# Spreading gamma over the partitions of an RMSNorm-Swish kernel with a TensorE product in place of a shuffle

## The chip, the cores and the metric

The kernel runs on one core of one Trainium2 chip. The metric is device microseconds of one execution, the median over runs. The granted TensorE clock is 1.0, and every profile is one profiled execution. In the profiles SP, ACT, DVE, POOL and PE are SyncE, ScalarE, VectorE, GpSimd and TensorE; an engine name with a q, as ACTq, is its queue of issued work.

## The reference

```python
batch, seq, dim = 16, 1024, 512          # x: 16 x 1024 x 512 float32, gamma: 512 ones, eps 1e-5
def reference(x, gamma, eps):
    rms = np.sqrt(np.mean(x ** 2, axis=-1, keepdims=True) + eps)
    x_norm = x / rms * gamma
    return (x_norm * (1.0 / (1.0 + np.exp(-x_norm)))).astype(np.float32)
```

33.56 MB are read and 33.56 MB are written.

## The kernel before

The 16384 rows lie 128 to a partition. They are cut into 11 tiles of 4 to 16 rows for each partition, in a ring of 96 rows, and into 32 chunks of 4 rows. For each chunk ACT squares (one row with a running sum, three into PSUM), DVE sums those three, POOL adds eps and takes the power -1/2 into `rstd`, DVE scales the four rows by `rstd` and gamma, and ACT applies Silu in place. SP issues the loads, ACT the stores.

```python
    sizes = [4, 4, 8] + [16] * 6 + [8, 8]
    ring = 96
    cn = 4                                        # rows of a chunk
    # ...
    gamma4 = sbuf("gamma4", [P, D])
    gamma_sb = sbuf("gamma_sb", [P, D])
    sq = [nc.alloc_psum_tensor(f"sq{i}", [P, 4, D], fp32).ap() for i in range(2)]
    # ... POOL
    nc.gpsimd.memset(gamma4, 0.0).then_inc(s_zero, 1)
    # ... for each chunk: the add (aeps), then the power (rstd)
    # ... ACT: the scratch write, then gamma into partitions 0, 32, 64 and 96
    need(nc.scalar.dma_start(out=scratch, in_=blank), s_blank, 1).then_inc(s_scratch, 16)
    need(
        nc.scalar.dma_start(out=gamma4[0:P:32, :], in_=gamma.partition_broadcast(4)),
        s_zero, 1,
    ).then_inc(s_gld, 16)
    # ... DVE
    for k in range(K + 1):
        if k < K:
            sums(k)
        if k == 0:
            need(nc.vector.stream_shuffle(gamma_sb, gamma4, [0] * 32), s_gld, 16
            ).then_inc(s_gamma, 1)
        if k == 1:
            nc.vector.wait_ge(s_gamma, 1)
        if k >= 1:
            norm(k - 1)                           # four scalings, the first waits for rstd
```

## Time and profile before

| | before |
|---|---|
| time | 160.27 us median (160.11 to 160.32) |
| span of the profiled execution | 158.7 us |
| DVE, ACT, POOL busy | 87%, 79%, 41% |
| the two DMA queues, share of the 16 engines | 49.9% + 49.3% |
| gamma lands, first scaling | 11.01, 13.31 us |
| last store issued, landed | 150.11, 158.66 us |

The time of a run is some 1.36 us longer than the landing of its last store (160.02 for the profiled execution, 158.66 its last landing).

### The profile page before, as it was taken

What the parts mean: (1) busy time and instruction counts of PE and PEld (TensorE: products, weight loads), DVE (VectorE), ACT (ScalarE), POOL (GpSimd) and SP (SyncE); (2) the same over time, 40 slices, a digit from 0 to 9 for tenths busy, and PEclk for the clock granted to TensorE, in tenths of its full rate; (3) what the DMA queues carried; (4) which work ended last, traced back from release to release, by engine and by line L of the source; (5) the groups of instructions that cost most, each with busy time, mean ns of one, the idle gap of its engine ahead of it and who ended that gap; (6) DMA issues with size and microseconds to landing.
All of it is one profiled execution on the core that took longest, in us unless ns stands there. A gap on an engine that the chain in (4) does not pass through costs nothing.

```text
span 158.7 us, 439 instructions
## 1 busy us (share of the span) xinstructions
DVE 138.9 (87%) x162; ACT 125.3 (79%) x129; POOL 65.4 (41%) x71
## 2 busy tenths in 40 slices
DVE  0249999999999999999999999999999999999300
ACT  0935989888888889988888888888998888883600
POOL 2035444444455555544444445555544444445000
DMA  7999999999999999999999999999999999999997
GB/s 235 427 523 405 396 450 419 409 452 407 460 394 413 467 421 452 413 396 479 432 413 429 446 429 413 425 417 458 429 454 396 434 446 438 446 413 438 388 458 301
DMA packets 3324, 67.15 MB, mean 423 GB/s; under 512 B 501, under 2 KB 501, under 8 KB 505
## 3 DMA queue, kind: packets, MB, share of 16 engines
q1 hardware_dynamic: 1584, 33.56, 49.9%
q10 hardware_dynamic: 1736, 33.57, 49.3%
q14 instruction: 4, 0.02, 0.0%
HBM read 33.56 MB, written 33.56 MB: 423 GB/s over the span
## 4 chain that ended last, share of the span: by engine, by line
DVE 85%; DMA 5%; ACT 1%; issue 1%; POOL 0%; POOLq 0%
DVE xb L224 53%; DVE ms L213 32%; DMA gamma<-in_gamma_dram 5%; ACT xb L184 1%; DVE gamma_sb L237 0%; POOL gamma L142 0%; POOL blank L141 0%; POOLq L65 0%
## 5 line engine op out<-in xcount | busy, mean ns | idle before, releaser
L224 DVE SCALAR_TENSOR_TENSOR xb<-xb,rstd,gamma_sb 128x512 f32<-128x512 f32 x128 | 87.4, 748 | 0.0
L184 ACT ACTIVATE xb<-xb 128x2048 f32<-128x2048 f32 x32 | 61.1, 1909 | 17.8 <-DVE xb L224 17.8
L213 DVE TENSOR_REDUCE ms<-sq 128x3 f32<-128x1536 f32 x32 | 56.1, 1754 | 7.0 <-ACT sq L172 7.0
L147 POOL TENSOR_SCALAR aeps<-ms 128x4 f32<-128x4 f32 x32 | 20.6, 644 | 75.2 <-DVE ms L213 75.2
L172 ACT ACTIVATE sq<-xb 128x1536 f32<-128x1536 f32 x32 | 45.9, 1433 | 0.0
L154 POOL TENSOR_TENSOR rstd<-aeps,neg_half 128x4 f32<-128x4 f32 x32 | 44.0, 1376 | 2.7
L165 ACT ACTIVATE junk<-xb 128x512 bf16<-128x512 f32 x32 | 19.7, 615 | 3.4 <-DMA xb<-in_x_dram 3.3
L165 ACT ACTIVATION_READ_ACCUMULATOR junk<-xb 128x1 f32 x32 | 6.0, 186 | 0.0
L199 ACT ACT_TABLE_LOAD x1 | 1.3, 1283 | 3.6 <-issue 3.6
L237 DVE LOAD_MASK_SELECT gamma_sb<-gamma x1 | 0.0, 14 | 2.3 <-DMA gamma<-in_gamma_dram 2.3
L141 POOL MEMSET blank<- 128x16 f32 x1 | 0.1, 111 | 1.5 <-POOLq L65 1.5
L237 DVE STREAM_SHUFFLE gamma_sb<-gamma 128x512 f32<-128x512 f32 x1 | 0.7, 717 | 0.0
L142 POOL MEMSET gamma<- 128x512 f32 x1 | 0.5, 524 | 0.0
L264 POOL MEMSET const-float32-0.0<- 128x1 f32 x1 | 0.1, 98 | 0.2 <-issue 0.2
L264 POOL MEMSET const-bfloat16-1.0<- 128x1 bf16 x1 | 0.1, 102 | 0.0
L264 POOL MEMSET const-uint8-127<- 128x1 uint8 x1 | 0.1, 101 | 0.0
L143 POOL MEMSET neg_half<- 128x4 f32 x1 | 0.1, 101 | 0.0
L264 POOL MEMSET const-float32-1.0<- 128x1 f32 x1 | 0.1, 98 | 0.0
## 6 DMA issues: line engine op xcount, KB each, us to landing
xb<-in_x_dram SPq DMA_DIRECT2D x6, 4096.0 KB, 41.9
out_dram<-xb ACTq DMA_DIRECT2D x6, 4096.0 KB, 31.1
xb<-in_x_dram SPq DMA_DIRECT2D x3, 2048.0 KB, 35.0
out_dram<-xb ACTq DMA_DIRECT2D x3, 2048.0 KB, 10.7
xb<-in_x_dram SPq DMA_DIRECT2D x2, 1024.0 KB, 5.8
out_dram<-xb ACTq DMA_DIRECT2D x2, 1024.0 KB, 20.8
scratch<-blank ACTq DMA_DIRECT2D x1, 8.0 KB, 7.7
gamma<-in_gamma_dram ACTq DMA_DIRECT2D x1, 8.0 KB
```

Source lines behind the costliest of these rows:

```text
L141: nc.gpsimd.memset(blank, 0.0).then_inc(s_blank, 1)
L142: nc.gpsimd.memset(gamma4, 0.0).then_inc(s_zero, 1)
L147: nc.gpsimd.tensor_scalar(out=aeps[:, k, :], in0=ms[:, k, :], scalar1=eps_f, scalar2=None, op0=ALU.add,),
L154: nc.gpsimd.tensor_tensor(out=rstd[:, k, :], in0=aeps[:, k, :], in1=neg_half, op=ALU.pow),
L165: acc = nc.scalar.activation(out=junk[k % 2], in_=xb[:, at + n_sq, :], func=AF.Square, scale=inv_d**0.5, accum_out=ms[:, k, n_sq : n_sq + 1],)
L172: square = nc.scalar.activation(out=sq[k % 2][:, 0:n_sq, :], in_=xb[:, at : at + n_sq, :], func=AF.Square, scale=inv_d**0.5,)
L184: nc.scalar.activation(out=rows, in_=rows, func=AF.Silu), s_norm, k + 1
L199: nc.scalar.preload_act_table_set("silu_and_others")
L213: nc.vector.tensor_reduce(out=ms[:, k, 0:n_sq], in_=sq[k % 2][:, 0:n_sq, :], op=ALU.add, axis=mybir.AxisListType.X,),
L224: ins = nc.vector.scalar_tensor_tensor(out=row, in0=row, scalar=rstd[:, k, j : j + 1], in1=gamma_sb, op0=ALU.mult, op1=ALU.mult,)
L237: nc.vector.stream_shuffle(gamma_sb, gamma4, [0] * 32), s_gld, 16
L264: nc = _bacc.Bacc("TRN2", target_bir_lowering=False, num_devices=1)
```

## The change

Its intent: gamma is fetched once and not four times, POOL no longer zeroes a 128x512 tile ahead of the transfer, and the spread over the partitions is a product of a column of ones with the row of gamma, written to the fourth row of a PSUM buffer of which the squares use three, and copied out by DVE.

```diff
-    gamma4 = sbuf("gamma4", [P, D])
+    gamma1 = sbuf("gamma1", [1, D])
+    ones = sbuf("ones", [1, P])
...
-    nc.gpsimd.memset(gamma4, 0.0).then_inc(s_zero, 1)
+    nc.gpsimd.memset(ones, 1.0).then_inc(s_one, 1)
...
-    need(
-        nc.scalar.dma_start(out=gamma4[0:P:32, :], in_=gamma.partition_broadcast(4)),
-        s_zero, 1,
-    ).then_inc(s_gld, 16)
+    nc.scalar.dma_start(out=gamma1, in_=gamma.unsqueeze(0)).then_inc(s_gld, 16)
...
+    spread = sq[1][:, 3, :]
+    nc.tensor.wait_ge(s_one, 1)
+    need(
+        nc.tensor.matmul(spread, lhsT=ones, rhs=gamma1, start=True, stop=True),
+        s_gld, 16,
+    ).then_inc(s_spread, 1)
...
-                nc.vector.stream_shuffle(gamma_sb, gamma4, [0] * 32), s_gld, 16
+                nc.vector.tensor_copy(out=gamma_sb, in_=spread), s_spread, 1
```

(Declarations of semaphores are left out.)

More of the change, by code (lines that the diff above doesn't have):

```diff
@@ L86 @@
     s_gld = nc.alloc_semaphore("s_gld")
-    s_zero = nc.alloc_semaphore("s_zero")
+    s_one = nc.alloc_semaphore("s_one")
+    s_spread = nc.alloc_semaphore("s_spread")
     s_half = nc.alloc_semaphore("s_half")
```

## The prediction

> **What bounds the kernel now.** I read the page first (busy times and the 40 slices), then the chain of waits that ended last, then the timeline of the start, then the DMA issues and the stretches at the end.
>
> ```profile
> span 158.7 us, 439 instructions
> DVE 138.9 (87%) x162; ACT 125.3 (79%) x129; POOL 65.4 (41%) x71
> ...
> DMA  7999999999999999999999999999999999999997
> ...
> q1 hardware_dynamic: 1584, 33.56, 49.9%
> q10 hardware_dynamic: 1736, 33.57, 49.3%
> ```
>
> There are two candidates for the bound. DVE is busy for 87% of the span. The 16 DMA engines are busy too: the two queues (q1 the loads, q10 the stores, the scratch write and gamma) add up to 99.2% of their time, and no slice after the first is below nine tenths. The chain of waits names DVE:
>
> ```profile
> 2.50 8.51 DMA gamma<-in_gamma_dram
> 11.01 0.03 issue
> 11.04 0.72 DVE gamma_sb L237 x2
> 11.76 0.06 DVE ms L213
> 11.82 1.49 issue
> 13.31 2.73 DVE xb L224 x4
> ...
> 142.84 5.31 DVE xb L224 x8
> 148.15 0.02 issue
> 148.17 1.91 ACT xb L184
> ```
>
> The reader is to see that gamma opens this chain. The transfer is issued at 2.50 and lands at 11.01; the shuffle over the partitions (0.72) follows at once; then come the second reduction and the first scaling at 13.31, and from there DVE runs without a pause (its groups show 0.0 us idle before the scalings) to 148.15. By this view whatever is added between 11.01 and 13.31 arrives at the end one for one.
>
> But the chain ends with the last Silu at 150.08, and the span ends 8.6 us later. What lies there is the last store, and the DMA issues, asked for by stretch (130 to 140, 140 to 150, 150 to 155 us), show that it waits in a queue:
>
> ```profile
> out_dram<-xb ACTq DMA_DIRECT2D x1, 4096.0 KB, 14.5
> ...
> out_dram<-xb ACTq DMA_DIRECT2D x1, 2048.0 KB, 10.7
> ...
> out_dram<-xb ACTq DMA_DIRECT2D x1, 2048.0 KB, 8.6
> ...
> 145.00:150.00 5.00, 3.14 (x5) 3.74 (x2) 0.06 (x1) 1.00 0.92 393
> ...
> 152.00:154.00 2.00, 0.00 (x0) 0.00 (x0) 0.00 (x0) 1.00 1.09 467
> 154.00:156.00 2.00, 0.00 (x0) 0.00 (x0) 0.00 (x0) 1.00 1.03 442
> ```
>
> (The last number of a DMA issue is the time from issue to landing; the last two of a stretch are the DMA share and GB/s.) The timeline has these three stores issued at 134.52, 143.15 and 150.11, so they land at 149.0, 153.85 and 158.7. The last two gaps are 4.85 us each for 2.10 MB, which is 432 GB/s, the rate of the whole run. So each store starts when the one before it is through, and the DMA engines, never idle since about 1 us, are what sets the end. The DVE chain runs close beside them with a little slack: in the packet records of the trace the last store's first data starts between 152.69 and 153.43 on the different engines, 2.6 to 3.3 us after its issue at 150.11. Some of that is start-up: the very first load, which had no queue before it, was issued at 0.00 and its first packet starts at 1.00. I estimate 1.0 to 1.5 us for the store[...]. The slack of the DVE chain is then 2.6 - 1.5 = 1.1 us at least and 3.3 - 1.0 = 2.3 at most, 1.7 in the middle.
>
> [...] q10 has 1736 packets, which is 11 stores of 128 + 16, the scratch write of 128 + 16, and 8 left for gamma, 4 of data and 4 of completion[...]. [...] The kernel before has no TensorE instruction[...].
>
> **The change part by part.** *Removed:* the 128x512 memset on POOL (0.52 us, done at 2.47) and the wait of the gamma transfer on it. It held the issue back by about 0.1 us (the scratch issue ends at 2.39, gamma's starts at 2.50). *The issue itself* took 1.10 us on ACT against 0.34 for a store; one plain row may be cheaper, up to 0.76 us, but then ACT only waits for the first load (its first square starts at 4.93, that load landed at 4.80 by the semaphore record). Worth 0.1 us, and DVE waits for gamma later anyhow.
>
> *The landing* hardly moves. In the packet records gamma stands on each ring behind the scratch write, whose completion packets start at 9.17 to 9.39; gamma's data follow at 9.85 to 10.00 and its completions at 10.54 to 10.68, each with one 0.61 us packet of the loads in between. So it lands two turns behind scratch[...]. [...] scratch's spread over all 16 is 0.2 us. I take 11.0, give or take 0.3.
>
> *Added on the path:* the product. [...] *Replaced on the path:* the shuffle (0.72, and 0.01 for its mask) by a copy of 128x512 out of PSUM. One pass of DVE over 128x512 takes 0.72 to 0.75 in this trace, so I take 0.70: -0.03. The product writes the fourth bank of a buffer of which only three are used, so no square is held up.
>
> Sum on DVE: 0.0 + 2.1 - 0.03 = about +2.1 us; the first scaling starts at 15.4 in place of 13.31, and the last store is issued at 152.2 in place of 150.11.
>
> *At the end of the span:* loads do not depend on DVE until the ring of 96 rows is full, and both queues hold work without a break, so during the 2 us the engines carry loads instead of stores and total work is the same. The other late stores have more room: the 4096 KB one is issued at 134.52 and its predecessor lands at 139.3, the next is issued at 143.15 and its predecessor at 149.0. Only the last one is near: 2.1 of delay less 1.1 to 2.3 of slack leaves 0 to 1.0, in the middle 0.4. Result: 160.27 + 0.4 = 160.7 us.
>
> **The rivals.** (a) *One for one.* The chain of waits is right, the store costs the same 8.6 us after its issue, and the kernel goes to 160.27 + 2.1 = 162.4 us. For it: the chain itself. Against it: the 4.85 us rhythm of the last landings and the 99.2%. (b) *Fully absorbed:* start-up of a store is 1.0 us or less of those 2.6 and the product is at most 1.6 us; 160.2 to 160.3. For it: the middle of my slack is close to the delay. (c) *Faster:* gamma comes earlier. DVE sat idle for 2.26 us before the shuffle, and the first row of rstd was ready at 10.2, so DVE could gain up to some 2 us; but the DMA engines would not end earlier for it, so even this makes 160.2. The packet order speaks against it. (d) *Gamma in pieces:* if one row were cut into 4-byte pieces, 32 for each engine, every piece behind a load packet of 0.6 to 1.2 us, gamma would land 20 to 38 us late, far over any slack, and the kernel would take about 180 to 198. [...] I give it 2%.
>
> **Range and chances.** The bottom is DMA work that does not change, 160.0 with the scatter of 160.11 to 160.32; the top is rival (a), 162.4. Two per cent is 3.2 us, so slower than 163.5 needs a product of over 3 us with no slack, or (d): 0.03. Faster than 157.1 would need less DMA work: 0.01. Within 2%: 0.96.
>
> **What would show it.** In the changed profile: a gamma landing at 10.7 to 11.3; TensorE busy for 1.7 to 2.2 us in one place just after it; DVE's idle time before the copy up from 2.3 to about 4.4; first scaling near 15.4; last store issued near 152.2 and landing in 6.5 to 7 us in place of 8.6; DMA share of the two queues still 98 to 99%. If the last store still takes 8.6 us, or the landings before it move back by 2 us as well, the DMA bound is wrong and (a) right. If gamma lands beyond 12, the reading of the packet order is wrong.

The 432 and 423 GB/s are what the trace shows, and that no higher rate is possible it does not show. The sum was: 0.0 for the landing, 2.1 for the product, -0.03 for the copy, so +2.1 us on DVE; less 1.7 us of slack that is 0.4 us, and 160.27 + 0.4 = 160.7 us. The 2.1 us, and the 1.7 to 2.2 us under what would show it, no trace had shown by then; the profile after shows 2.08 us.

## More of the kernel before

The experiments ran on three chips, which their results number 0, 8 and 9; for the first measurement of the changed kernel the chip is not recorded. Each chip served one session, so chip and session can't be told apart.

One more group of before will be needed, POOL's add of eps (columns: busy us, mean ns of one, idle time before them):

```profile
L147 POOL TENSOR_SCALAR aeps<-ms 128x4 f32<-128x4 f32 x32 | 20.6, 644 | 75.2 <-DVE ms L213 75.2
```

It is an operation on four elements for each partition, and it takes 0.64 us in the mean. The first one, at a time when DVE is idle, takes 0.23.

## The result and the profile after

The changed kernel takes 161.18 us (160.84 to 161.37, four runs) against 160.27 (160.11 to 160.32). The ratio is 1.0056, with a 95% interval of 1.0037 to 1.0075: a small loss, clear of noise, inside the predicted range and 0.5 us above the predicted 160.7.

The head of the page and the two queues, after:

```profile
span 159.5 us, 443 instructions
...
PE 2.1 (1%) x2; PEld 0.5 (0%) x2; DVE 138.9 (87%) x161; ACT 125.2 (78%) x129; POOL 104.2 (65%) x71
...
q1 hardware_dynamic: 1584, 33.56, 49.7%
q10 hardware_dynamic: 1730, 33.57, 49.0%
```

The product is there with 2.1 us, no square of ACT waits for it (0.0 us idle before L174), DVE has as much work as before, and the DMA queues still fill 98.7% of the span. Two things are not as predicted. POOL is busy for 104 us in place of 65. And q10 has 1730 packets, which is 1728 for the stores and the scratch write and only 2 for gamma: one packet of 2048 bytes and one completion, so one engine carried it. The trace's record of the issue has gamma as 1x1 elements of 2048 bytes. In the kernel before it has 4x1, and gamma took 4 packets of 2048 bytes and 4 completions there.

The chain of waits after (start, duration, what), its beginning and its end:

```profile
2.43 8.18 DMA gamma<-in_gamma_dram
...
10.65 2.08 PE sq L213 x2
...
12.75 0.69 DVE gamma_sb L244
...
13.50 1.52 issue
...
142.89 1.68 DVE ms L220
...
144.64 2.66 POOL aeps L149
...
147.37 1.04 POOL rstd L156
...
148.44 2.75 DVE xb L231 x4
...
151.21 1.91 ACT xb L186
```

At the beginning the product takes 2.08 us and the copy 0.69, gamma landed 0.4 us earlier than before (10.60 in place of 11.01), and the first scaling starts at 15.03 in place of 13.31: +1.72. At the end something new has appeared. Before, the last eight scalings ran in one piece. Now the last four wait for POOL, whose add took 2.66 us; its group shows that this is no single case:

```profile
L149 POOL TENSOR_SCALAR aeps<-ms 128x4 f32<-128x4 f32 x32 | 68.3, 2133 | 39.8 <-DVE ms L220 39.8
```

By the timeline the first adds take 0.66 us, and from the ninth chunk on (45.4 us) each takes 2.65: it ends only when all four scalings that DVE runs meanwhile are over. Where a text below says that POOL is shut out, it means such an add of 2.65 us and nothing beyond it. In the middle of the kernel nobody waits for it, since `rstd` is needed one chunk later. At the end DVE has no reduction left to do, and the last scaling waits 1.24 us. So the last store is issued at 153.15, 3.04 us later than before: 1.72 from the start, 1.24 from POOL, and 0.08 of small change.

The end of the span after, by stretches (the last two columns are DMA share and GB/s), and the last store's line:

```profile
150.00:152.00 2.00, 0.00 (x0) 0.00 (x0) 1.18 (x2) 0.79 (x1) 0.00 (x0) 1.00 1.09 467
152.00:154.00 2.00, 0.00 (x0) 0.00 (x0) 0.00 (x0) 1.12 (x1) 0.00 (x0) 1.00 0.42 180
154.00:156.00 2.00, 0.00 (x0) 0.00 (x0) 0.00 (x0) 0.00 (x0) 0.00 (x0) 1.00 1.21 508
```

```profile
out_dram<-xb ACTq DMA_DIRECT2D x1, 2048.0 KB, 6.3
```

Between 152 and 154 us the DMA share falls to 0.42: here, and only here, the engines have run out of work (they run dry) and wait for the last store to be issued. (A packet counts where it begins, so a share above 1 in the next stretch is no error.) In the packet records all 16 engines begin that store between 153.99 and 154.14, together, 0.84 to 0.99 us after its issue; before, they began it one by one, from 152.69 to 153.43, as each was through with the store ahead. The store lands 6.3 us after its issue in place of 8.6. Of 3.04 us of delay, 2.2 were absorbed in its queue and 0.82 reached the end (159.48 in place of 158.66).

### The profile page after: what moved, and what is told of

It reads as the page before. It is cut to its first block, busy times and chain, and to the rows that moved or that the text cites. A ratio compares the mean times of both kernels' runs of the same rounds, so it can differ in the third digit from the quotient of the medians.

```text
span 159.5 us, 443 instructions
## 1 busy us (share of the span) xinstructions
PE 2.1 (1%) x2; PEld 0.5 (0%) x2; DVE 138.9 (87%) x161; ACT 125.2 (78%) x129; POOL 104.2 (65%) x71
## 3 DMA queue, kind: packets, MB, share of 16 engines
q10 hardware_dynamic: 1730, 33.57, 49.0%
## 4 chain that ended last, share of the span: by engine, by line
DVE 83%; DMA 5%; POOL 2%; PE 1%; issue 1%; ACT 1%; ACTq 0%; POOLq 0%
DVE xb L231 52%; DVE ms L220 31%; DMA gamma<-in_gamma_dram 5%; POOL aeps L149 2%; PE sq L213 1%; ACT xb L186 1%; POOL rstd L156 1%; DVE gamma_sb L244 0%; ACTq L194 0%; POOL blank L143 0%; POOLq L65 0%
## 5 line engine op out<-in xcount | busy, mean ns | idle before, releaser
L149 POOL TENSOR_SCALAR aeps<-ms 128x4 f32<-128x4 f32 x32 | 68.3, 2133 | 39.8 <-DVE ms L220 39.8
L231 DVE SCALAR_TENSOR_TENSOR xb<-xb,rstd,gamma_sb 128x512 f32<-128x512 f32 x128 | 88.6, 785 | 1.2 <-POOL rstd L156 1.2
L220 DVE TENSOR_REDUCE ms<-sq 128x3 f32<-128x1536 f32 x32 | 57.2, 1789 | 7.0 <-ACT sq L174 7.0
L174 ACT ACTIVATE sq<-xb 128x1536 f32<-128x1536 f32 x32 | 45.9, 1433 | 0.0
L156 POOL TENSOR_TENSOR rstd<-aeps,neg_half 128x4 f32<-128x4 f32 x32 | 35.5, 1110 | 2.7
L244 DVE COPY gamma_sb<-sq 128x512 f32<-128x512 f32 x1 | 0.7, 692 | 4.0 <-PE sq L213 4.0
L213 PE MATMUL sq<-gamma,ones 1*128 1x512 f32 x2 | 2.1, 1136 | 10.6 <-DMA gamma<-in_gamma_dram 10.6
L213 PEld LDWEIGHTS sq<-gamma,ones 1*128 1x128 f32 x2 | 0.5, 304 | 10.6 <-DMA gamma<-in_gamma_dram 10.6
```

Of the source, the lines that this page charges most:

```text
L149: nc.gpsimd.tensor_scalar(out=aeps[:, k, :], in0=ms[:, k, :], scalar1=eps_f, scalar2=None, op0=ALU.add,),
L156: nc.gpsimd.tensor_tensor(out=rstd[:, k, :], in0=aeps[:, k, :], in1=neg_half, op=ALU.pow),
L174: square = nc.scalar.activation(out=sq[k % 2][:, 0:n_sq, :], in_=xb[:, at : at + n_sq, :], func=AF.Square, scale=inv_d**0.5,)
L213: nc.tensor.matmul(spread, lhsT=ones, rhs=gamma1, start=True, stop=True),
L220: nc.vector.tensor_reduce(out=ms[:, k, 0:n_sq], in_=sq[k % 2][:, 0:n_sq, :], op=ALU.add, axis=mybir.AxisListType.X,),
L231: ins = nc.vector.scalar_tensor_tensor(out=row, in0=row, scalar=rstd[:, k, j : j + 1], in1=gamma_sb, op0=ALU.mult, op1=ALU.mult,)
```

## The experiments

The slack is the time by which the last store may be issued later before the end of the kernel moves. The theory: two limits set the end. One is the DMA work, which ends at about 158.7 to 159.2 whatever DVE does. The other is the issue of the last store plus 6.34 us. The rivals: DVE's chain alone (every delay arrives), or scatter of the DMA engines alone. The POOL stall needs an explanation of its own. In the tables "issue" is the issue of the last store in the profiled execution, "landing" its landing.

### The changed kernel again (chip 9)

No edit.

> The changed kernel once more, unedited, to see whether what its first profile shows besides the product is steady: from 45 us on the 4-wide add on POOL takes 2.65 us in place of 0.66, so the last scaling waits 1.24 us for POOL. Theory: the end is the later of two limits, the DMA work (160.3 us) and the issue of the last store + 6.33 us + 1.34 us from span to time; with the last store issued at 153.15 that gives 160.8, and 161.0 to 161.3 is expected with the POOL stall again. Rival: the stall is an accident of one profile; then the last store is issued near 151.9 and the time is 160.3 to 160.4.

160.81 us (160.56 to 160.87) against 160.25. Nobody waits for POOL here: all adds take 0.66 us. Gamma landed at 11.00, the first scaling started at 15.42, the last store was issued at 152.24 and landed at 159.19. The stall of the first profile is therefore not a steady part of the change. The engines never ran dry:

```profile
150.00:152.00 2.00, 0.00 (x0) 0.00 (x0) 0.27 (x1) 1.70 (x1) 0.00 (x0) 1.00 1.01 434
152.00:154.00 2.00, 0.00 (x0) 0.00 (x0) 0.00 (x0) 0.21 (x1) 0.00 (x0) 1.00 1.07 459
```

The expectation is missed all the same: I had 160.3 to 160.4 for the case without the stall, and it is 160.8. The packet records say what the half microsecond is. An engine's packets took 157.67 us in sum against 157.40 in the first profile of before, and the engines lost 1.36 us at the very start (until 2 us) against 1.18. Both are time of the DMA engines, not of the DVE chain. This call's ratios have wide intervals (here 0.9948 to 1.0065), because one of the runs of before took 162.21 us; I compare medians. On this chip alone the half microsecond is therefore not apart from the noise. On chip 8 it is: the changed kernel with a later add (below), which has the same start and no stall either, has a ratio of 1.0028 (1.0011 to 1.0046).

### The kernel before with a product on its path (chip 9)

```diff
+    nc.tensor.matmul(sq[1][:, 3, :], lhsT=ones, rhs=gamma4[0:1, :], ...)   # waits for gamma, sets s_spread
-  nc.vector.stream_shuffle(gamma_sb, gamma4, [0] * 32), s_gld, 16
+  nc.vector.stream_shuffle(gamma_sb, gamma4, [0] * 32), s_spread, 1
```

> The kernel before with the product put on the path (the shuffle waits for a product whose result nobody reads); transfer, shuffle and all addresses stay as before. Theory: gamma lands at 11.0, first scaling at 15.3 to 15.5, last store issued at 152.2 without the POOL stall (time 160.3 to 160.4) or at 153.4 to 153.5 with it (time 161.0 to 161.3). The stall here would say that the later start brings it, its absence that the addresses or the copy in place of the shuffle do. Rival (the chain of waits alone sets the end): 162.4 in any case.

160.70 us (160.31 to 161.12) against 160.25. First scaling 15.51, issue 152.33, landing 159.28, no stall; the time is 0.3 us above the expected 160.3 to 160.4, as in the repeat. The one ingredient, a product of 2.1 us on the path, brings the whole shift of the start and the same time as the changed kernel on the same chip (160.81). Transfer, copy and addresses play no part that this run can see. The rival of one for one (162.4) is out.

### Half of the scalings left out (chip 9)

```diff
-        for j in range(cn):
+        for j in range(2):
```

> The changed kernel with only two of the four scalings of each chunk (wrong results on purpose): some 42 us of work less on DVE. Theory that the DMA engines set the end: ACT's work of some 127 us is next and ends near 140, the stores queue up, and the time stays at 160.0 to 160.6. Rival that the DVE chain sets it: ends with ACT, 148 to 152.

An edit of the changed kernel. 160.18 us (160.06 to 161.47) against 160.25. Its output is wrong, which doesn't matter for the time. The head of the page:

```profile
PE 2.1 (1%) x2; PEld 0.5 (0%) x2; DVE 99.2 (62%) x97; ACT 123.2 (77%) x129; POOL 65.0 (41%) x71
```

DVE lost 40 us of work, the last store was issued at 143.15, seven microseconds earlier than before, and it landed 15.75 us later at 158.90, with the kernel no faster. So DVE does not set the end here, and the DMA engines, without a gap from 2 us on, do. For the kernel before, which has the same loads and stores, issues its last store later and lands it at 158.66 to 158.95, the same follows, although its chain of waits gives DVE 85%.

### Gamma ahead of the scratch write (chip 8)

```diff
+    nc.scalar.dma_start(out=gamma1, in_=gamma.unsqueeze(0)).then_inc(s_gld, 16)
     need(nc.scalar.dma_start(out=scratch, in_=blank), s_blank, 1).then_inc(
         s_scratch, 16
     )
-    nc.scalar.dma_start(out=gamma1, in_=gamma.unsqueeze(0)).then_inc(s_gld, 16)
```

> The changed kernel with gamma issued ahead of the scratch write. Gamma no longer stands behind nine packets of scratch on its ring and lands at 6 to 8 us, the product is done before or soon after the first reduction (8.75), first scaling near 11.1 to 11.5, last store issued at 147.9 to 148.5, some 2 us earlier than before. Theory that the DMA engines set the end: time 160.1 to 160.5, no gain over before. Rival that the DVE chain sets it: 158.0 to 158.3.

160.28 us (160.09 to 160.56) against 160.31. Gamma landed at 6.64, which shows that the 11 us came from its place behind scratch on the queue, and the first scaling started at 11.15, 2.2 us earlier than before. The time is as predicted, but the last store was issued at 150.76, not at 148. The timeline shows where the head start went (the bracket is the idle time and what ended it):

```profile
12.34 0.63 ACT L167 ACTIVATE junk<-xb 128x512 bf16<-128x512 f32 x1 [2.90 <-DMA xb<-in_x_dram]
...
23.14 0.63 ACT L167 ACTIVATE junk<-xb 128x512 bf16<-128x512 f32 x1 [2.35 <-DMA xb<-in_x_dram]
```

The wait for the third load stood in the kernel before too (2.96 us at 12.33). The wait for the fourth, 2.35 us, is new; ACT and DVE behind it lose most of the head start there. So serving gamma faster only moves the wait of the chain from gamma to the loads.

### The kernel before again (chip 8)

No edit.

> The kernel before, unedited, as a control with a second profile. Expected: last store issued at 150.1, DMA engines without a gap between 2 and 156 us, time 160.1 to 160.4. If its packets take as long in all as those of the repeat of the changed kernel (157.67 us per engine against 157.40 in the first profile of before), the half microsecond between them that is not idle time is scatter of the DMA engines; if they stay at 157.4, a late start of the stores makes the packets slower.

160.26 us (160.01 to 160.39) against 160.31 for the same code; issue 150.10, landing 158.95, no stall, no gap of the engines from 2 us on. Its packets took 157.12 us for each engine, after a start that lost 1.49. Start and packets together are 158.58 and 158.61 us in the two profiles of before, and 159.03 in the repeat of the changed kernel. In the repeat, with its later start of the stores, the packets of the loads took 0.14 to 0.35 us more in sum than in these two; I come back to it.

### The product twice (chip 8) and three times (chip 0)

```diff
     need(
         nc.tensor.matmul(spread, lhsT=ones, rhs=gamma1, start=True, stop=True),
         s_gld, 16,
-    ).then_inc(s_spread, 1)
+    )
+    nc.tensor.matmul(
+        spread, lhsT=ones, rhs=gamma1, start=True, stop=True
+    ).then_inc(s_spread, 1)
```

> The changed kernel with the product done twice in a row: its cost on the path doubled. Theory: the slack is used up, so the second 2.07 us arrives one for one from there on: first scaling at 17.2 to 17.5, last store issued at 154.2 to 154.4, landing 6.3 us later, time 161.8 to 162.1 (1.0 to 1.3 over the changed kernel of the repeat, as its last store had some 0.8 us of slack left). Rival without slack: 160.27 + 4.2 = 164.4. Rival that the whole difference is scatter of the DMA engines: 160.8.

> The product three times. The second one added 1.69 us to the first scaling, so last store issued at 153.91 + 1.7 = 155.6, landing 6.34 later at 161.95, time 163.2 to 163.4: 1.7 over the doubled product, one for one, as no slack is left. Rival that engines and chain overlap further: 162.4 or less.

Twice: 161.58 us (161.44 to 161.61) against 160.31, ratio 1.0080 (1.0063 to 1.0097). The second product delayed the first scaling by 1.69 us (17.11), less than the 2.07 that I had allowed for; why a product that follows another adds less, the run does not show. It took nearly 0.4 us off, and the time is 0.2 us below the expected 161.8 to 162.1. Issue 153.91, landing 160.25, which is 6.34 later. The engines ran dry for 0.9 us at the end, and for 0.8 us near 138 us, where they waited for the last 4096 KB store (issued at 138.32). That store too has only so much room. Of the 1.67 us by which the issue moved against the repeat, 1.06 arrived at the landing.

Three times: 164.61 us (164.47 to 164.70) against 160.13, ratio 1.0277. I had 163.2 to 163.4. First scaling 18.82 (+1.71, as expected), but issue 156.94 in place of 155.6: this run shows the POOL stall (20 long adds, 1.2 us of waiting for the last `rstd`), which I had left out since the doubled product on chip 8 had none. From the issue on the theory holds: 156.94 + 6.35 = 163.29, the measured landing. The unprofiled runs lie at the same 164.5 to 164.7, so the stall is no effect of profiling.

### The stall made on purpose, in both kernels (chip 0)

```diff
     for k in range(K):
+        if k == K - 1:
+            nc.gpsimd.wait_ge(s_norm, K - 1)
```

> The changed kernel with the POOL stall of its first profile made on purpose: the add of the last chunk waits until the scalings of the chunk before are done. Theory: the last scaling waits 1.4 to 1.6 us, last store issued at 153.6 to 153.9, landing 6.3 us later, time 161.2 to 161.5, some 0.6 over the changed kernel without the stall (160.8). Rival that nothing at the end of the DVE chain matters: 160.8.

> The same stall in the kernel before. Theory: last store issued at 151.5 to 151.8, and 6.3 us later is 158.0, earlier than the DMA engines are through (158.7 to 159.0): time 160.1 to 160.4, as before. Rival that a delay of the DVE chain always costs something: 160.9 or more.

In the changed kernel: 161.62 us against 160.13, 0.1 above the expected range; issue 153.88, landing 160.23 (6.35 later). In the kernel before: 160.14 us against 160.13, issue 151.75, 1.6 us later than before, landing 159.13. The same stall costs nothing where the slack is whole and arrives where the product has used it up, which fits the account of the first profile, start plus stall less slack. One control is missing: the changed kernel without the edit was not run on chip 0, so its side is compared with the 160.81 of chip 9.

These two runs show something else that I had not asked for. In both, the adds become long by themselves, long before the forced stall. Here is the kernel before with the edit (line numbers are moved by 2):

```profile
L226 DVE SCALAR_TENSOR_TENSOR xb<-xb,rstd,gamma_sb 128x512 f32<-128x512 f32 x128 | 88.3, 774 | 1.5 <-POOL rstd L156 1.5
L149 POOL TENSOR_SCALAR aeps<-ms 128x4 f32<-128x4 f32 x32 | 48.0, 1500 | 55.0 <-DVE ms L215 51.8
```

1500 ns in the mean, and it is the gamma path of before, shuffle and all. So the long adds can come without the change.

### The add started later (chip 8)

```diff
     for k in range(K):
+        need(nc.gpsimd.memset(idle[:, k, :], 0.0), s_sum, k + 1)
         need(
             nc.gpsimd.tensor_scalar(
```

> The changed kernel with a one-element memset on POOL ahead of each add, so that the add starts some 0.1 us later, after the first scaling has begun. Theory: POOL is then shut out of every chunk (adds of 2.6 us in all chunks, not from the ninth on as in the first profile of the changed kernel), the last scaling waits 1.2 to 1.4 us, the last store is issued at 153.4 to 153.6, time 161.0 to 161.3, which is where the first four runs of the changed kernel were. Rival that the long adds came from something else than their start: adds stay at 0.66 us and the time at 160.8.

A miss. 160.68 us (160.44 to 161.03) against 160.31, and all adds stayed at 0.62 us, although they started 0.21 us after the first scaling had begun, later than the first long add of the first profile did (0.19). The start of the add alone does not decide. The memset ahead of it was on POOL at that time (from 0.14 us after the start of the first scaling, for 0.10 us), so the run is not clean enough to say more.

### A wait for POOL at the tail (chip 9)

```diff
-            if j == 0:
+            if j == 0 and k == K - 2:
+                need(ins, s_eps, K)
+            elif j == 0:
                 need(ins, s_rstd, k + 1)
```

> The changed kernel; the four scalings of the chunk before the last wait until POOL has done the add of the last chunk, so that POOL isn't shut out during them. Theory: 0.3 us lost there, 1.24 us of waiting for POOL gone, last store issued at 152.1 to 152.3, time 160.3 to 160.5. Rival: the stall at the end costs nothing and the 0.9 us come from the start or from the DMA engines; then 161.1 as the changed kernel.

160.50 us (160.22 to 160.59) against 160.25, and 160.81 for the changed kernel on this chip. The run can't answer its question, since this chip shows no stall: the wait added 0.44 us of delay (issue 152.68, landing 159.12) and removed nothing. It is one more point for the second limit, because 152.68 + 6.34 is 159.02 and the engines ran dry for 0.27 us. By the medians it is 0.3 us faster than the unedited kernel, but the two profiled executions differ by 0.07 (160.49 and 160.56), and their packets by 0.13 (157.54 us against 157.67). I take the 0.3 for scatter; that is not shown.

### A shorter last store (chip 0)

```diff
-    sizes = [4, 4, 8] + [16] * 6 + [8, 8]
+    sizes = [4, 4, 8] + [16] * 6 + [8, 4, 4]
```

> The changed kernel with the last tile of 8 rows split into two of 4, so that the last store is half as large and the other half is issued 4.3 us earlier. Theory: the last store needs some 3.9 us from issue to landing with idle engines, 152.24 + 3.9 = 156.1 is long before the DMA work is through, so the slack is back: time 160.2 to 160.7, the rest over before being the packets' own scatter (0.1 to 0.5 us). It can't beat before. Rival: 160.8 to 161.2 as the changed kernel.

The expected 3.9 us is an estimate, 6.34 less 1.05 MB at 432 GB/s; the run does not test it. 160.96 us (160.74 to 161.12) against 160.13, ratio 1.0049: a miss. The slack was back, as meant: the last store, issued at 153.51 with the stall in it, met engines that had work to the end (no gap from 2 us on) and took 6.3 us. But the packets took 158.13 us for each engine, 0.73 more than in the first profile of before. 0.1 of it is the larger number of 8 KB packets: on each engine 16 packets of 16 KB become 32 of 8 KB, and in the profile of before these take 0.611 and 0.309 us. Most of the rest is in packets of loads, 32 KB each, between 80 and 90 us, some of which took 2.0 to 2.2 us in place of 1.21; the last of the loads were being issued at that time. So this remedy at the tail did not bring the time back to that of before. What it gains over the changed kernel on this chip is not known, since that one was not run there.

### What the runs say together

| run | chip | first scaling | issue | landing | landing - issue | engines dry at the end |
|---|---|---|---|---|---|---|
| before | - | 13.31 | 150.11 | 158.66 | 8.55 | no |
| before again | 8 | 13.30 | 150.10 | 158.95 | 8.85 | no |
| before, stall | 0 | 13.32 | 151.75 | 159.13 | 7.38 | no |
| half of the scalings | 9 | 15.34 | 143.15 | 158.90 | 15.75 | no |
| gamma first | 8 | 11.15 | 150.76 | 158.74 | 7.98 | no |
| after again | 9 | 15.42 | 152.24 | 159.19 | 6.95 | no |
| later add | 8 | 15.41 | 152.22 | 159.15 | 6.93 | under 0.1 us |
| before, product | 9 | 15.51 | 152.33 | 159.28 | 6.95 | 0.1 us |
| wait at the tail | 9 | 15.42 | 152.68 | 159.12 | 6.44 | 0.3 us |
| after | - | 15.03 | 153.15 | 159.48 | 6.33 | 0.8 us |
| after, stall | 0 | 15.45 | 153.88 | 160.23 | 6.35 | 1.5 us |
| product twice | 8 | 17.11 | 153.91 | 160.25 | 6.34 | 0.9 us, and 0.8 near 138 |
| product three times | 0 | 18.82 | 156.94 | 163.29 | 6.35 | 2.2 us, and 2.5 near 138 |

(The run with the shorter last store is left out, since its store is of another size.) Where all engines run dry, for 0.8 us or more, the last store takes 6.33 to 6.35 us in four kernels whose delays differ by nearly 4 us. Where they don't, or only some do for 0.1 to 0.3 us, it takes longer and the landing stays between 158.7 and 159.3, whether its issue is at 143 or at 152. The two limits cross near 152.4 to 152.8 (158.7 to 159.2 less 6.34). The kernel before issues at 150.1, some 2.3 us ahead of the lower value.

No version beats the kernel before. The gamma-first version ties with it (160.28 against 160.31), as it must where the DMA work is the limit.

## Why the prediction was right

*The DMA bound:* right, and shown by the run with half of the scalings. (One reading is loose: the last of the 40 DMA slices is at seven tenths, not nine; the packets end there.)

*The product, 2.1 us:* 2.07 to 2.08 in every profile with one product, at a granted clock of 1.0, in two recorded matmuls (1.06 and 1.22 us in the first profile); a second and a third product added 1.69 and 1.71. So the sum was right; its parts no trace shows. *The copy, 0.70:* 0.69.

*The landing of gamma at 11.0, give or take 0.3:* 10.60 in the first profile, 10.91 to 11.03 in every later run of the changed kernel and its variants behind scratch. The reading of the order in the queue was right; gamma moved to 6.64 when it was put ahead. The step about several engines was wrong: one packet of 2048 bytes on one engine carried the row. It hardly mattered for the landing. The same packet rules out rival (d).

*+2.1 us on DVE, last store at 152.2:* the repeat has +2.11 and 152.24. In the first profile it is +1.72 and 153.15. What failed there is that the prediction had nothing happen between the start and the end of the chain; the POOL stall of 1.24 us did.

*Slack of 1.1 to 2.3 us:* 2.2 in the first pair (8.55 less 6.33), at the top of the range, because the start-up of a store on idle engines, which I had put at 1.0 to 1.5 us, is 0.84 to 0.99 in the first profile of the changed kernel. The 1.0 was the first load's, in the profile of before; the 1.5 was my allowance, which no trace showed.

*0.4 us in sum:* 0.9 measured in the first set, 0.55 in the repeat (160.81 against 160.25). That the end is the later of the DMA work and the chain was right; two terms were missing, and that 160.7 comes so near is partly luck. With the measured slack of 2.2 us the prediction's own sum lets the 2.1 us vanish and gives 160.3. In the first set the missing term is the stall, without which the issue would have been at 151.9 and inside the slack. In the repeat, where the engines never ran dry, it is the statement that the total DMA work stays the same. It stays the same in bytes, but start and packets together took 158.58 and 158.61 us for each engine before, and 158.77 to 159.03 in the five runs on chips 8 and 9 that start the scalings between 15.3 and 15.5. The product done twice, with its start at 17.1, has 158.72, so it is no steady growth with the delay. The longer packets are loads, mostly around 24 to 32, 47 to 51 and 81 to 85 us. No run isolates what makes them longer; it stays open.

*The POOL stall* could not have been read from the profile before, where no add takes more than 0.66 us. There an add of 0.23 us on its own takes 0.66 when a scaling has just begun, and ends just after that scaling. It is the same on chips 8 and 9: no add takes more than 0.66 us, in all eight profiles (with the memset ahead of it, 0.62). On chip 0, in all four profiles, it comes at some point to take until the fourth scaling is over (2.64 to 2.65 us in the run with the shorter last store). In those four, and in the first profile of the changed kernel, DVE's scalings begin ever earlier in the record relative to the end of the one before, so that the recorded duration of one grows from 741 to 743 ns at the start to 809 to 823 at the end, at an unchanged pace of 0.66 us from start to start; the long adds set in when it has reached 762 to 772. On chips 8 and 9 it never exceeds 774; the two ranges overlap, so this duration alone does not decide. What holds the add, for one scaling or for four, is not shown, and why the durations grow in some sessions and not in others is open. The change is not needed for it: the kernel before with its own gamma path does it as well on chip 0. Whether the change makes it likelier is not shown. In the first measurement only the changed kernel has it, and on chip 0 it sets in at the 18th chunk of the kernel before and at the 9th to 13th of the changed one. In the kernel before the stall is hidden by the slack, as its time of 160.14 us on chip 0, with a forced stall, shows.

## What to carry to other kernels

A chain of waits that names one engine for 85% of the span does not prove that this engine sets the end. Look at what lies after the chain, and compare the time from issue to landing of the last stores with what such a store needs on idle engines; the difference is the slack (here 8.55 less 6.33 us), and a small one-off cost is free up to it and is paid in full beyond it. When two resources are both nearly full, expect a change on one of them to arrive in part, and budget for what else eats the same slack on another chip (here 1.2 us of waiting for POOL on chip 0).
